# A pooling and latent-attention trunk: the attention's three engines in the order of the program text, with the projections cut into fine pieces

## The chip, the cores and the metric

The kernel runs on one core of one Trainium2 chip. The time is device microseconds of one execution; the median of some runs is compared. A core has TensorE (PE, matmuls and transposes), VectorE (DVE), ScalarE (ACT), GpSimd (POOL), SyncE (SP, which here only issues DMAs), an on-chip memory, and eight PSUM banks that matmuls write. Each engine executes its own list of instructions in the order in which the compiled program holds them; engines wait for each other by semaphores.

## What is computed

Two layers on 512 tokens of 2048 features, in float32. The first is a gated pooling mixer, which this change leaves as it is. After it come keys and values from a compressed latent of 512 and, from its own latent of 512, the queries of 16 heads of 128 + 64 features (the 64 are rotated by position):

```
q, k = qk_norm_rope(q, q_norm_g), qk_norm_rope(k, k_norm_g)   # per head: over 192 features
for i in range(4):                                            # query blocks of 128
    s = q[block i] @ k[: (i + 1) * 128].T * 192 ** -0.5       # chunks of 64 masked
    o[block i] = softmax(s) @ v[: (i + 1) * 128]
x = x + (o * silu(gate)) @ w_out
```

qk_norm_rope divides each token's 192 features by their root mean square. Block i sees i + 1 blocks of keys, so the work of a head grows from block 0 to block 3.

## The kernel before, in words

Every float32 operand is split in two parts of a faster type, hi (a cast, ScalarE) and lo (the difference, VectorE), and each product is three matmuls: hi hi, hi lo, lo hi. Weights are split too: `load_w` (line 118) loads 256 KB into one of three `raw` buffers (SP's queue) and makes a `whi` and a `wlo`, of which there are four each.

The mixer takes the first 1200 us or so. Then come the latents (`latent`, `latent_norm`), 16 gate projections (`gate_unit`, 599: 48 matmuls of 512 columns, Silu, the result kept in an `at` tile until its head is done), and the attention in eight head groups of two heads.

A group's preparation (`prep_units`, 813), in pieces with short names: B loads the k and v weights; k0 to k3 (`kv_unit`) make raw keys and values of four token blocks, 12 matmuls of 512 each; K (`kstats_unit`) makes the keys' reciprocal roots from sums of squares and scales the raw keys; q0 to q3 (`q_unit`, 12 matmuls of 384) make the raw queries; S (`qstats_unit`) their reciprocal roots. T0 to T5 (`tr_unit`, 709) are transposes of four 128 x 128 blocks into one PSUM bank each, which ScalarE and VectorE then empty with a cast and a difference: T0 and T1 the keys of two heads, T2 their rotated part (two banks), T3 and T4 the queries, T5 their rotated part.

The group's attention (`attn_units`, 826) has eight blocks (two heads, four blocks). `score_unit` (750) is five matmuls into a score bank, a mask (MEMSET), the maximum over the row, the exponential with its sum (ScalarE), a reciprocal and a scaling (VectorE). `pt_unit` (775) transposes the block's probabilities into a transpose bank and splits them; `pv_unit` (792) multiplies by v after every second block, and after the head's last one VectorE multiplies by the gate (line 811), into the gate's tile. `og_unit` splits a gated head, `out_unit` and `out_store` are the last projection.

PSUM: three banks `mm`, two `sc`, two `tr` (T0 to T5 and the probabilities' transposes take them in turn) and one `ov`.

The order around the attention: `main` is the list of blocks, `fill` the preparation of the next group (in the last group: parts of the last projection), and LEAD and PACE set how they mix. The program text is then reordered by a scheduler, which decides what stands where on each engine:

```
PREP = "B k0 k1 k2 k3 K q0 q1 T0 T2 q2 T1 q3 T3 T4 S T5".split()
...
        mpos += [hg + x / len(au) * PACE for x in range(len(au))]
...
        due += [hg + (x + 1) / n - LEAD for x in range(n)]
...
    while j < len(fill) and due[j] <= mpos[i]:
```

Of the kernel before, what the change touches and what calls it, by code (L numbers as in the profile page):

```python
# [43 lines left out]

PREP = "B k0 k1 k2 k3 K q0 q1 T0 T2 q2 T1 q3 T3 T4 S T5".split()

LEAD = 0.421
PACE = 1.091
# [3 lines left out]
def trunk_kernel(  # L52
# [27 lines left out]
    def at(dt=F32R):  # L80
        return apool.tile([P, S], dt, tag="a", name="at")
# [348 lines left out]
    xpool = ctx.enter_context(tc.tile_pool(name="xpool", bufs=16, **tile_))  # L430
# [35 lines left out]
    for g in range(NG):  # L466
# [11 lines left out]
        for o in range(KD):  # L478
            first = len(wloads)
            acc = proj(awo[g, o], 8, ys)  # L480
            if g == 0:
                x = xt()
# [117 lines left out]
    def gate_unit(o):  # L600
# [3 lines left out]
        sg = at(F32)  # L604
        A.activation(sg, z, AF.Silu)
        gates.append(sg)
# [5 lines left out]
    st = {}  # L612
# [4 lines left out]
    def hg_begin(hg):  # L617
        d = {}
        d["kvw"] = [load_w(wkvb[hg, :, k * 512:(k + 1) * 512], 512) for k in range(4)]
        d["kraw"] = [xt((P, 2, 256)) for _ in range(2)]  # L620
        d["qraw"] = [None] * 4
        vt = bt if hg else xt
        d["vh"] = [vt((P, 2, 256), F32R) for _ in range(2)]
        d["vl"] = [vt((P, 2, 256), F32R) for _ in range(2)]
# [4 lines left out]
    def kv_unit(hg, t):  # L629
        d = st[hg]  # L630
        acc = mm()
        tsl = slice(t * P, (t + 1) * P)
        for k in range(4):
            hi, lo = d["kvw"][k]
            ch, cl_ = cn[k]
            T.matmul(acc, ch[:, tsl], hi, start=(k == 0), stop=False)  # L636
            T.matmul(acc, cl_[:, tsl], hi, start=False, stop=False)  # L637
            T.matmul(acc, ch[:, tsl], lo, start=False, stop=(k == 3))  # L638
        a, b = t // 2, t % 2
        A.copy(d["kraw"][a][:, b, :], acc[:, 0:256])  # L640
        split(acc[:, 256:512], d["vh"][a][:, b, :], d["vl"][a][:, b, :])
        for h in range(2):
            junk = spool.tile([P, 192], mybir.dt.bfloat16, tag="junk", name="junk", bufs=2)
            A.activation(junk[:, 0:128], d["kraw"][a][:, b, h * P:(h + 1) * P], AF.Square,
                         accum_out=d["ssk"][:, 2 * t + h:2 * t + h + 1])

    def q_unit(hg, t):
        d = st[hg]
        if t == 0:
            d["qw"] = [load_w(wqb[hg, :, k * 384:(k + 1) * 384], 384) for k in range(4)]  # L650
        acc = mm()
        tsl = slice(t * P, (t + 1) * P)
        for k in range(4):
            hi, lo = d["qw"][k]
            qh, ql_ = qn[k]
            T.matmul(acc[:, 0:384], qh[:, tsl], hi[:, 0:384], start=(k == 0), stop=False)  # L656
# [156 lines left out]
    def prep_units(hg):  # L813
        def q(t):
            q_unit(hg, t)
            qrot_unit(hg, t)
# [154 lines left out]
```

## Time and profile before

| | us |
|---|---|
| median of three runs | 1948.48 (1948.02 to 1948.8) |
| the profiled execution | 1946.78 |
| its span, first to last instruction | 1945.0 |
| TensorE busy | 1920.2 |
| VectorE busy | 1276.3 |
| ScalarE busy | 822.6 |

The attention lies between 1500 and 1800 us of the span. In a row of the timeline the columns are start, duration, engine, line, operation, tiles (out<-in) and shapes; in square brackets the idle time of that engine just before and what ended it. A group row of the instructions ends in busy time, mean duration in ns, and idle time before. A row of the chain of waits is start, length, what. A row of a stretch has its length and each engine's busy time (instructions): PE, weight loads, DVE, ACT, POOL, then granted clock, DMA share and GB/s. A matmul's row shows its whole passage; the next one starts before it ends.

### The profile page before, as it was taken

The page shows a single profiled execution, that of the slowest core. Times are in us where ns is not written, and L with a number is a line of the kernel's source. Part 1 is how long each engine was busy: PE and PEld are TensorE (multiplying, and loading weights), DVE is VectorE, ACT ScalarE, POOL GpSimd, SP SyncE. Part 2 cuts the span into 40 slices and gives each one's busy share as a digit, 9 for nine tenths or more (in the row PEclk, how much of TensorE's full clock was granted, in tenths as well). Part 3 has the DMA queues.
Part 4 walks back from the last instruction along what each step waited for, and adds up shares of the span by engine and source line. Part 5 has one row for each costly group of instructions (what it writes and reads, how often), then busy time and mean ns, then how long its engine had stood idle before and what let it go on. Part 6 is the DMA issues. An engine that isn't in the chain of part 4 may idle for free.

```text
span 1945.0 us, 30576 instructions
## 1 busy us (share of the span) xinstructions
PE 1920.2 (99%) x11356; PEld 1707.8 (88%) x11356; DVE 1276.3 (66%) x2297; ACT 822.6 (42%) x1570; POOL 252.5 (13%) x404
## 2 busy tenths in 40 slices
PE   8999999999999999999999999999999999999999
PEld 8999999999999977888888888888888888888887
DVE  8677785896666687585685567473344888796432
ACT  7433433333333433333323454332244777785221
POOL 0423333343223000000000000000010111110000
PEclk9999999999999999999999999999999999999999
DMA  6545444344444446334334343333322111121632
GB/s 189 162 153 163 149 134 129 123 134 136 148 141 144 149 161 199 118 124 141 121 123 141 114 145 121 93 93 98 97 93 71 56 39 55 47 67 51 215 119 87
DMA packets 168006, 235.53 MB, mean 121 GB/s; under 512 B 14768, under 2 KB 95024, under 8 KB 167856
## 3 DMA queue, kind: packets, MB, share of 16 engines
q1 hardware_dynamic: 167568, 233.37, 37.8%
q8 instruction: 89, 1.46, 0.3%
q14 instruction: 61, 0.50, 0.1%
q10 hardware_dynamic: 288, 0.20, 0.0%
HBM read 208.35 MB, written 25.17 MB: 120 GB/s over the span
## 4 chain that ended last, share of the span: by engine, by line
PE 88%; DVE 4%; DMA 3%; ACT 3%; issue 1%; SPq 0%; POOL 0%; DVEq 0%; ACTq 0%; POOLq 0%
PE mm L147 14%; PE mm L146 14%; PE mm L145 14%; PE k L338 10%; PE k L334 10%; PE k L336 10%; PE sc L762 2%; PE mm L636 2%; PE mm L638 1%; PE mm L637 1%; PE mm L656 1%; PE mm L657 1%; PE mm L658 1%; PE tr L732 1%; DVE wlo L128 1%
## 5 line engine op out<-in xcount | busy, mean ns | idle before, releaser
L127 ACT CAST whi<-raw 128x512 fp32r<-128x512 f32 (+2 forms) x421 | 252.6, 608 | 505.2 <-PE mm L146 438.5
L334 PE MATMUL k<-xc,hi 128*128 128x256 f32 x1680 | 460.0, 283 | 0.0
L336 PE MATMUL k<-xc,hi 128*128 128x256 f32 x1680 | 460.0, 283 | 0.0
L128 DVE TENSOR_TENSOR wlo<-raw,whi 128x512 fp32r<-128x512 f32 (+2 forms) x421 | 281.4, 672 | 229.3 <-ACT whi L127 228.1
L338 PE MATMUL k<-xc,lo 128*128 128x256 f32 x1680 | 417.8, 283 | 1.1 <-DVE lo L316 1.0
L315 ACT CAST hi<-raw 128x1792 fp32r<-128x1792 f32 x120 | 202.7, 1689 | 363.0 <-PE k L338 246.2
L316 DVE TENSOR_TENSOR lo<-raw,hi 128x1792 fp32r<-128x1792 f32 x120 | 246.7, 2056 | 159.4 <-ACT hi L315 159.2
L147 PE MATMUL mm<-bt,wlo 128*128 128x512 f32 x860 | 335.9, 391 | 1.3 <-DVE wlo L128 1.3
L145 PE MATMUL mm<-bt,whi 128*128 128x512 f32 x860 | 334.9, 389 | 0.6 <-ACT bt L150 0.6
L146 PE MATMUL mm<-bt,whi 128*128 128x512 f32 x860 | 334.5, 389 | 0.0
L334 PEld LDWEIGHTS k<-xc,hi 128*128 128x128 f32 x1680 | 322.5, 192 | 0.0
L336 PEld LDWEIGHTS k<-xc,hi 128*128 128x128 f32 x1680 | 322.5, 192 | 0.0
L338 PEld LDWEIGHTS k<-xc,lo 128*128 128x128 f32 x1680 | 296.8, 192 | 2.0 <-DVE lo L316 1.5
L147 PE MATMUL mm<-at,wlo 128*128 128x512 f32 x516 | 201.3, 390 | 1.5 <-DVE wlo L128 1.5
L146 PE MATMUL mm<-at,whi 128*128 128x512 f32 x516 | 202.0, 392 | 0.2 <-DVE at L150 0.2
L145 PE MATMUL mm<-at,whi 128*128 128x512 f32 x516 | 200.7, 390 | 0.0
L147 PEld LDWEIGHTS mm<-bt,wlo 128*128 128x128 f32 x860 | 161.4, 188 | 36.7 <-DVE wlo L128 2.9
L145 PEld LDWEIGHTS mm<-bt,whi 128*128 128x128 f32 x860 | 161.4, 188 | 34.6 <-ACT bt L150 1.0
L146 PEld LDWEIGHTS mm<-bt,whi 128*128 128x128 f32 x860 | 161.4, 188 | 33.7 <-DVE bt L150 0.2
L311 POOL TENSOR_TENSOR raw<-raw 128x256 f32<-128x256 f32 x120 | 97.0, 808 | 436.4 <-DVE raw L309 413.4
L147 PEld LDWEIGHTS mm<-at,wlo 128*128 128x128 f32 x516 | 96.9, 188 | 22.5 <-DVE wlo L128 2.7
L146 PEld LDWEIGHTS mm<-at,whi 128*128 128x128 f32 x516 | 96.9, 188 | 21.3 <-DVE at L150 1.4
(1149 smaller groups left out, 2588.2 us busy)
## 6 DMA issues: line engine op xcount, KB each, us to landing
raw<-awin SPq DMA_DIRECT2D x240, 256.0 KB, 3.2
raw<-awo SPq DMA_DIRECT2D x128, 256.0 KB, 2.9
raw<-bwin SPq DMA_DIRECT2D x80, 256.0 KB, 2.8
raw<-awg SPq DMA_DIRECT2D x64, 256.0 KB, 2.7
raw<-bwo SPq DMA_DIRECT2D x59, 256.0 KB, 2.8
scr<-e SPq DMA_DIRECT2D x56, 256.0 KB, 2.7
raw<-wkvb SPq DMA_DIRECT2D x32, 256.0 KB, 2.9
raw<-wqb SPq DMA_DIRECT2D x32, 192.0 KB, 2.4
```

What stands on the lines that cost most here:

```text
L127: A.copy(hi[:, :n], raw[:, :n])
L128: V.tensor_tensor(lo[:, :n], raw[:, :n], f(hi[:, :n]), ALU.subtract)
L145: T.matmul(dst, wh, xh, start=first, stop=False)
L146: T.matmul(dst, wh, xl, start=False, stop=False)
L147: T.matmul(dst, wl, xh, start=False, stop=last)
L311: G.tensor_tensor(c[:, :, 6, :], c[:, :, 4, :], c[:, :, 2, :], ALU.add)
L315: A.copy(hi, c[:, :, 1:8, :])
L316: V.tensor_tensor(lo, c[:, :, 1:8, :], f(hi), ALU.subtract)
L334: T.matmul(dst, hi[:, j % 2, wi, :], xh[j][:, xi, :], start=first, stop=False, skip_group_check=True)
L336: T.matmul(dst, hi[:, j % 2, wi, :], xl[j][:, xi, :], start=False, stop=False, skip_group_check=True)
L338: T.matmul(dst, lo[:, j % 2, wi, :], xh[j][:, xi, :], start=False, stop=last, skip_group_check=True)
L636: T.matmul(acc, ch[:, tsl], hi, start=(k == 0), stop=False)
```

## The change

1. **The order.** After the first 14 gates, every instruction of TensorE, ScalarE and VectorE is bound behind the one that stands before it in the program text (`add_manual_dep`), so that the scheduler can't move it on its engine. DMAs and GpSimd aren't bound.
2. **The pieces.** k0 to q3 are cut into four pieces each (one weight chunk, three matmuls), the exponential, the scaling and the sums of squares become steps of their own. A list `prep_items` lays down the preparation; `fill_to` deals its pieces between the score blocks by time shares (0.35 and 0.7 of a block's slot), and continues without a break from one group into the next. K and S stay one piece each. Gates 14 and 15 are pieces of group 0's preparation, parts of the last projection those of the end.
3. **Weights.** A chunk is loaded and split in the text when the fourth last chunk was used for the last time.
4. **Buffers and DRAM.** The 16 `x` buffers are divided into 11 and 5 for queries; raw k and v use the `at` pool. A gate is stored to DRAM after its Silu, loaded two blocks before its head ends, multiplied, stored again (not for the last group) and loaded once more for its split: four transfers of 256 KB a head.

```diff
+    def kv_part(hg, t, k, w):
...
+        if k == 3:
+            a, b = t // 2, t % 2
+            split(acc[:, 256:512], d["vh"][a][:, b, :], d["vl"][a][:, b, :])
+            A.copy(d["kraw"][a][:, b, :], acc[:, 0:256])
...
+        first = [k(0, i) for i in range(4)]
+        for t in range(1, 4):
+            first += [k(t, 0), k(t, 1), kq(t - 1), k(t, 2), k(t, 3)]
...
+        first += [q(0, 0), q(0, 1), kq(3), q(0, 2), q(0, 3), piece(0, kstats_unit, hg),
+                  q(1, 0), q(1, 1), qq(0), q(1, 2), q(1, 3), kr(0), tr_(0), qq(1), tr_(1),
...
+        return (first + nxt[:2] + [qq(3), piece(0, qstats_unit, hg), tr_(3)] + nxt[2:3] + [tr_(4)] +
+                nxt[3:4] + [tr_(5)] + nxt[4:])
...
+    def fill_to(us):
+        nonlocal pos, done
+        while pos < len(fill) and done + fill[pos][0] / 2 <= us:
+            t, w, fn, a = fill[pos]
+            if w is None:
+                fn(*a)
+            else:
+                key = (fn, a[0], a[2]) if fn in (kv_part, q_part) else (fn,) + a
+                fn(*a, parts[key])
+            split_due(pos)
+            done += t
+            pos += 1
...
+    for m in range(len(seq) + 2):
+        now = seq[m] if m < len(seq) else None
+        if now:
...
+            score_unit(*now)
+        if m >= 2 and seq[m - 2][2] % 2:
+            pv_unit(*seq[m - 2][:2], seq[m - 2][2] // 2)
+        if now:
+            fill_to(at_ + share * 0.35)
+            exp_unit(*now)
+        if 1 <= m <= len(seq):
+            pt_unit(*seq[m - 1])
+        if now:
+            fill_to(at_ + share * 0.7)
+            scale_unit(*now)
+            fill_to(at_ + share)
...
+    for ins in block[begin:]:
+        e = ins.engine
+        if e in (mybir.EngineType.PE, mybir.EngineType.Activation, mybir.EngineType.DVE):
+            if e in prev:
+                tc.add_manual_dep(ins, prev[e].name, mybir.DependencyInfo(
+                    mybir.DependencyClass.NoSync, mybir.DependencyReason.DATA), reason="order of the pieces")
+            prev[e] = ins
```

What this does to the engines' lists is shown at three places of one head group in the middle; the other groups read alike. First VectorE before, at the end of the key statistics (`sy` is the reciprocal root, the eight rows of line 679 scale the raw keys, `sc` is a score bank, `nm` the maximum, `tr` a transpose bank):

```order
L164 SCALAR_TENSOR_TENSOR sy<-sa,sy 128x8
L679 TENSOR_SCALAR xt<-xt,sy 128x128 x8
L811 TENSOR_TENSOR at<-ov,at 128x512
L771 RECIPROCAL sm<-sm 128x1
L772 TENSOR_SCALAR tt__15897<-tt__15897,sm 128x128
L771 RECIPROCAL sm<-sm 128x1
L772 TENSOR_SCALAR tt__15935<-tt__15935,sm 128x256
L150 TENSOR_TENSOR bt<-tr,bt 128x512
```

and VectorE now, from the same step on:

```order
L163 SCALAR_TENSOR_TENSOR sy<-sa,sy 128x8
L692 TENSOR_SCALAR at<-at,sy 128x128 x8
L788 MEMSET sc 64x64
L790 TENSOR_REDUCE nm<-sc 128x1
L792 SCALAR_TENSOR_TENSOR nm<-nm,qy 128x1
L149 TENSOR_TENSOR xt<-tr,xt 128x2x128
L149 TENSOR_TENSOR xt<-tr,xt 128x128
L149 TENSOR_TENSOR bt<-tr,bt 128x512
L806 RECIPROCAL sm<-sm 128x1
L807 TENSOR_SCALAR tt__16571<-tt__16571,sm 128x512
L149 TENSOR_TENSOR bt<-tr,bt 128x512
```

The maximum of block 3 of the first head (L790) and the split of block 2's probabilities (the two L149 into `xt`) stand behind the scalings now; before, they stood elsewhere. ScalarE at the same place now (L800 is an exponential, L700 the rotated keys):

```order
L800 ACTIVATE tt__15415,sm<-sc,nm,qy 128x512
L149 CAST xt<-tr 128x2x128
L149 CAST xt<-tr 128x128
L670 COPY qt<-mm 128x384
L700 ACTIVATE tt__15439<-krr,sy 128x128 x4
L149 CAST bt<-tr 128x512
```

The cast of block 2's probabilities follows block 3's exponential, and T0's cast follows both. TensorE before, around one of these transposes (L732 is T0, T1, T3, T4 or T5, L656 to L658 the q projection):

```order
L656 MATMUL mm<-whi,at 128x384
L732 MATMUL tr<-cs,xt 128x128
L657 MATMUL mm<-whi,at 128x384
L732 MATMUL tr<-cs,xt 128x128
L658 MATMUL mm<-wlo,at 128x384
L732 MATMUL tr<-cs,xt 128x128 x2
L656 MATMUL mm<-whi,at 128x384
```

and TensorE now (L815 are the transposes of block 2's probabilities, L753 T0 and T1, L787 the scores of the second head's block 0):

```order
L815 MATMUL tr<-cs,tt__16485 128x128 x3
L664 MATMUL mm<-whi,at 128x384
L665 MATMUL mm<-whi,at 128x384
L666 MATMUL mm<-wlo,at 128x384
L753 MATMUL tr<-cs,at 128x128 x8
L787 MATMUL sc<-bt 128x128 x5
```

T0 and T1 are eight transposes in a row now, one q piece behind block 2's. And TensorE now at T3 and T4 (both L753):

```order
L753 MATMUL tr<-cs,qt 128x128 x4
L815 MATMUL tr<-cs,tt__16746 128x128 x2
L641 MATMUL mm<-whi,at 128x512
L642 MATMUL mm<-whi,at 128x512
L643 MATMUL mm<-wlo,at 128x512
L753 MATMUL tr<-cs,qt 128x128 x4
L641 MATMUL mm<-whi,at 128x512
```

Between T3 and T4 stand a block's two transposes and one k piece of the next group; the query statistics stand on VectorE between that block's scaling and T3's difference.

More of the change, by code (lines that the diff above doesn't have):

```diff
@@ L652, in q_unit @@
         tsl = slice(t * P, (t + 1) * P)
[L653 to L656, printed above, removed]
[L657 to L661 removed]
+        hi, lo = w
@@ new lines, in trunk_kernel, with split_due @@
+    for m, (key, w) in enumerate(keys):
+        n = last[keys[m - 4][0]] if m >= 4 else -1
+        assert n < use[key]
+        due.setdefault(n, []).append((key, w))
+    parts = {}
+    def split_due(n):
+        for key, w in due.get(n, ()):
+            parts[key] = load_w(*w)
+    block = nc.cur_bb.bb.instructions
+    begin = len(block)
+    split_due(-1)
+    pos, done = 0, 0.0
+    def fill_to(us):
[4 more added lines that the diff above has]
+                fn(*a)
+            else:
+                key = (fn, a[0], a[2]) if fn in (kv_part, q_part) else (fn,) + a
+                fn(*a, parts[key])
+            split_due(pos)
+            done += t
+            pos += 1
```

280 lines of the change are left out of this document (171 added, 109 removed).

## The prediction

> **What bounds the kernel now.** I read the page first, then the chain of waits, then TensorE's own rows. The page's busy line, and its slices:
>
> ```profile
> PE 1920.2 (99%) x11356; PEld 1707.8 (88%) x11356; DVE 1276.3 (66%) x2297; ACT 822.6 (42%) x1570; POOL 252.5 (13%) x404
> ...
> DVE  8677785896666687585685567473344888796432
> ...
> PEclk9999999999999999999999999999999999999999
> ```
>
> TensorE is the bound everywhere, and VectorE comes near it in the attention (0.7 to 0.9 in slices 32 to 36 of 40). The chain of waits passes TensorE once in each head group at the same place, so it shows the length of one group:
>
> ```profile
> 1584.04 2.02 PE sc L762 x10
> ...
> 1622.07 2.02 PE sc L762 x10
> ```
>
> A group takes 38.0 us. The stretch view says of one group:
>
> ```profile
> 1584.00:1622.00 38.00, 37.01 (x222) 32.66 (x221) 31.18 (x112) 28.37 (x98) 6.00 (x16) 1.00 0.16 50
> ```
>
> TensorE is busy for 37.0, VectorE for 31.2, ScalarE for 28.4 of 38.0 us. By busy time only 1.0 us could be won. But a matmul's row reaches past the start of the next. So I count starts: of 512 columns, 384, 256, and four transposes.
>
> ```profile
> 1608.20 0.39 PE L636 MATMUL mm<-whi,at 128*128 128x512 f32 x1
> 1608.42 0.39 PE L637 MATMUL mm<-whi,at 128*128 128x512 f32 x1
> ...
> 1613.79 0.33 PE L657 MATMUL mm<-whi,at 128*128 128x384 f32 x1
> ...
> 1615.70 0.33 PE L658 MATMUL mm<-wlo,at 128*128 128x384 f32 x1
> ...
> 1617.10 0.28 PE L806 MATMUL ov<-xt,bt 128*128 128x256 f32 x1
> ...
> 1617.69 0.28 PE L808 MATMUL ov<-xt,bt 128*128 128x256 f32 x1
> ```
>
> ```profile
> 1518.01 0.60 PE L732 MATMUL tr<-cs,xt 128*128 128x128 f32 x4
> 1518.36 0.60 PE L762 MATMUL sc<-bt 128*128 128x256 f32 x3
> ```
>
> That is 0.23, 0.174 (11 steps), 0.118 (5 steps), and 0.35 for four transposes. A group has 48 matmuls of 512 for k and v (10.9), 48 of 384 for q (8.3), the scores with 5 each of 128 to 512 for two heads (6.3), 36 for probabilities times v (4.0) and 48 transposes (4.2): 33.7 us. So **4.4 us** of each group's 38.0 are lost between starts. They lie in one stretch of 8 us, where no projection is left to run beside the softmax:
>
> ```profile
> 1600.68 0.39 PE L762 MATMUL sc<-bt 128*128 128x512 f32 x1
> 1601.31 0.55 PE L762 MATMUL sc<-bt 128*128 128x128 f32 x3 [0.24 <-ACT tt__16221 L770]
> ...
> 1605.37 0.28 PE L806 MATMUL ov<-xt,bt 128*128 128x256 f32 x1
> 1605.90 0.38 PE L807 MATMUL ov<-xt,bt 128*128 128x256 f32 x1 [0.25 <-DVE xt L150]
> ```
>
> 0.63 us stands where 0.23 would do, and 0.53 for 0.12. [...]
>
> **What the change removes.** It deals projection pieces evenly between the score blocks. If that worked without side effects it would win 4.4 us in each of seven groups, some 31 us, and a few more at both ends.
>
> **What it adds.** The three engines now run in the order of the program text. The statistics are one piece each there, and VectorE has nothing between their steps:
>
> ```profile
> 1614.28 0.16 DVE L162 TENSOR_TENSOR sa<-sy 128x8 f32<-128x8 f32 x1
> 1614.47 0.17 DVE L163 TENSOR_TENSOR sa<-sa,sv 128x8 f32<-128x8 f32 x1
> ...
> 1615.27 0.17 DVE L164 SCALAR_TENSOR_TENSOR sy<-sa,sy 128x8 f32<-128x8 f32 x1
> 1615.47 1.66 DVE L679 TENSOR_SCALAR xt<-xt,sy 128x128 f32<-128x128 f32 x8
> ```
>
> Steps that wait for each other start 0.20 us apart (1614.28 to 1615.27 is five of them). The key statistics have 11 such steps (2.2), four small additions before them (some 0.5) and eight scalings (1.66): 4.4 us. The query statistics have 12 steps: 2.4 us. Other durations, of one group, come from the groups of instructions with their shapes:
>
> ```profile
> L150 ACT CAST xt<-tr 128x256 fp32r<-128x256 f32 x8 | 3.0, 376 | 0.5 <-PE tr L781 0.5
> ...
> L150 ACT CAST xt<-tr 128x128 fp32r<-128x128 f32 x4 | 1.1, 264 | 1.2 <-PE tr L781 1.2
> ```
>
> ```profile
> L150 DVE TENSOR_TENSOR xt<-tr,xt 128x256 fp32r<-128x256 f32 x8 | 3.3, 416 | 0.3 <-ACT xt L150 0.3
> ...
> L150 DVE TENSOR_TENSOR bt<-tr,bt 128x512 fp32r<-128x512 f32 x3 | 2.1, 693 | 1.2 <-ACT bt L150 1.2
> ...
> L745 DVE SCALAR_TENSOR_TENSOR bt<-tr,gqk,bt 128x512 fp32r<-128x512 f32 x2 | 1.5, 746 | 0.1
> ...
> L765 DVE TENSOR_REDUCE nm<-sc 128x1 f32<-128x512 f32 x2 | 1.4, 678 | 0.0
> ...
> L767 DVE SCALAR_TENSOR_TENSOR nm<-nm,qy 128x1 f32<-128x1 f32 x8 | 1.2, 146 | 0.0
> ...
> L150 DVE TENSOR_TENSOR xt<-tr,xt 128x128 fp32r<-128x128 f32 x4 | 1.1, 284 | 0.0
> ...
> L765 DVE TENSOR_REDUCE nm<-sc 128x1 f32<-128x384 f32 x2 | 1.1, 554 | 0.0
> ```
>
> and from ScalarE's and VectorE's rows around one exponential:
>
> ```profile
> 1603.75 0.78 ACT L770 ACTIVATE tt__16282<-sc,nm,qy 128x512 f32<-128x512 f32 x1
> 1604.41 0.21 ACT L770 ACTIVATION_READ_ACCUMULATOR tt__16282<-sc,nm,qy 128x1 f32 x1
> 1604.50 0.37 ACT L150 CAST xt<-tr 128x256 fp32r<-128x256 f32 x1
> ```
>
> ```profile
> 1604.65 0.16 DVE L771 RECIPROCAL sm<-sm 128x1 f32<-128x1 f32 x1
> 1604.92 0.49 DVE L772 TENSOR_SCALAR tt__16282<-tt__16282,sm 128x512 f32<-128x512 f32 x1
> ```
>
> An exponential of 512 holds ScalarE for 0.75 us, and a handoff costs 0.03 (accumulator done at 1604.62, reciprocal at 1604.65). Now TensorE's new waits in a group, one by one.
>
> *T1, the second key transpose.* On TensorE it follows T0 at once. It needs the transpose bank that block 2's probabilities hold (there are two banks). These leave through ScalarE and VectorE, in turns, and both engines have other work ahead of that: VectorE the key statistics and then block 3's maximum, ScalarE block 3's exponential. T0 ends when the seventh scaling is done. From there: the eighth scaling 0.20, maximum 0.68, its scaling 0.15, exponential 0.75, cast 0.38, difference 0.42, second cast 0.26, difference 0.28 = 3.1, with handoffs **3.3 us** in which TensorE has nothing in its order. That holds however late the engines come. Low 3.1, high 3.5.
>
> *T0 itself.* From the end of block 2's scores TensorE has eight q pieces (24 x 0.174), block 3's scores (1.1), a product (0.65) and five block transposes (0.5): 6.4 us. VectorE and ScalarE need maximum 0.55 + 0.15, exponential some 0.66, cast 0.38, difference 0.42, reciprocal and scaling some 0.6, statistics until T0 4.2: 7.0, with handoffs 7.4. So 1.0 at least. And in VectorE's order the split of the fourth q weight stands ahead of that maximum:
>
> ```profile
> raw<-wqb SPq DMA_DIRECT2D x32, 192.0 KB, 2.4
> ```
>
> Its load waits for a raw buffer that the first q weight leaves (three buffers), which waits for the last use of the first k weight. Cast and split 0.5 each, 2.4 landing, 0.5 each again is 4.4 after a point that lies 2.8 before the end of block 2's scores: the maximum comes some 1.6 late. I take **2.6** (1.0 to 2.7), and 0.4 for the q piece that waits for that weight.
>
> *T4, the second query transpose.* It needs T3's bank; T3's difference stands behind the query statistics, and these behind block 2's maximum. Maximum 0.55 + 0.15, statistics 2.4, difference 0.75 and handoffs: 4.0 us, against two block transposes and one k piece on TensorE (0.9): **3.0** (2.3 if TensorE is late).
>
> *T2.* After block 3's scaling VectorE makes T1's difference (0.69), the maximum of 128 columns and its scaling (0.4), the exponential 0.45, then cast, difference, cast, difference (1.6): 3.2, 3.4 with handoffs, before a bank is free; TensorE has 1.2 of work. **2.1** (1.0 to 2.3).
>
> *Block 3's transposes*, twice a group: once behind T0's cast, 0.5; once behind T4, two T5 halves, k splits and its own exponential, some 9.4 us of alternating work against 7.0 on TensorE: 2.3. Together **2.8** (0 to 3).
>
> Sum per group: 3.3 + 2.6 + 0.4 + 3.0 + 2.1 + 2.8 = **14.2 us** lost in place of 4.4; bounds 7.8 and 15.5. Seven groups: 7 x 9.8 = +69.
>
> **The rest.** Projection of group 0 stands alone now, with gates 14 and 15 inside: statistics 4.4 against 2.1 us of q pieces before T0, and the query statistics once: some 4 us lost. I put the loss there now at 2, an estimate by the same count of starts: +2 (0 to +5). Group 7 with output pieces: such a piece is four weights long (2.7 us), VectorE's load is lighter; I give it and the ends -4 (-6 to +3), since the loss there now can go. DRAM trips: four transfers of 256 KB a group on queues that are 0.16 busy; a gate load is issued two blocks (8 us) before its product. Their cover is that lead; without it a landing, 2 to 3 us a head, would show, so 0 (0 to +10). The new buffers and the other order of cast and copy move nothing ahead of a matmul: 0.
>
> Sum: the profiled execution took 1946.78 us (span 1945.0 and 1.78 around it, 1.7 below the median). 1946.78 + 69 + 2 - 4 = 2013.8; I take **2012**, a little off for idle engines that answer sooner.
>
> **Rivals.** *Only the bounds hold* (18%). If T0, T2 and the block transposes wait little because the engines catch up, 7.8 a group remain: 7 x 3.4 = +24, 1970. Speaking for it: VectorE would be busy for only 31 of some 47 us.
>
> *The clock falls as well* (15%). At the start, after 5.8 us of idle time, 256 columns took 0.21 us instead of 0.12, and 4 us later still did:
>
> ```profile
> 5.80 0.58 PE L387 MATMUL k<-xc,hi 128*128 128x256 f32 x1 [5.80 <-ACT hi L150]
> ...
> 9.59 0.41 PE L388 MATMUL k<-xc,hi 128*128 128x256 f32 x1
> 9.80 0.41 PE L387 MATMUL k<-xc,hi 128*128 128x256 f32 x1
> ```
>
> Four us at that rate hold work for a little over two, so a fall costs some 2 us. T0's and T1's waits lie 0.35 us apart, 6 us of little work. One fall a group is 7 x 2 = +14: 2026. [...] No row here shows a fall in the middle of the kernel: the granted clock is in its highest tenth in every slice.
>
> *Faster* (11%). The even dealing wins and the waits stay under 4.4 us a group. This needs the statistics to be out of the way before TensorE comes to T0 and T3: VectorE would have to reach them 5 us sooner than worked out, and T1's wait would have to be a chain that I read wrongly. With 1 us left a group: 7 x -3.4 - 4 = 1919. For it: VectorE has 31 us of work for 33.7 on TensorE, so there is room on paper. Against it: the order is fixed, and VectorE can't go ahead in it. It decides at 4.4 us of waits a group.
>
> *The change cancels itself* (4%): waits of about 4.4, 1945.
>
> **Numbers.** Forecast 52%. A difference under 0.2% (3.9 us) is about what can't be told from none. Slower 52 + 18 + 15, and 1 of the last: 0.86; same 0.03; faster 0.11. The range leaves out the faster case and little above: bounds of the sum are 1960 and 2025, with the clock 2036: 1958 to 2036.
>
> **What would show it.** In the profile after: the distance of equal places of two groups near 47.5 us; rows of the second key transpose with over 3 us of idle time before, ended by VectorE's difference; TensorE's busy share in the attention down from 97% to some 75%; VectorE's busy time a group still 31 us; no change before the gates. I am wrong if groups take under 38 us, or if the waits are ended by DMAs.

## The result, and the profile after

| | before | after |
|---|---|---|
| median, us | 1948.25 (4 runs, 1947.73 to 1948.8) | 2057.89 (4 runs, 2056.18 to 2058.4) |
| span of the profiled execution | 1945.0 | 2055.7 |
| a head group in the steady part | 38.0 | 51.2 |

The ratio is 1.0561, with a 95% interval of 1.0543 to 1.0579: slower by 109.6 us. The forecast was 2012 with a range of 1958 to 2036. The direction was right, the size was not.

The page of the changed kernel, busy line, VectorE's slices and the granted clock:

```profile
PE 1961.6 (95%) x11356; PEld 1735.4 (84%) x11356; DVE 1300.5 (63%) x2297; ACT 828.0 (40%) x1570; POOL 253.0 (12%) x404
...
DVE  8677776886666774866845666533466666666432
...
PEclk9999999999999999999999999999989888889999
```

VectorE's slices in the attention (30 to 37 of 40) are at 0.6 where 0.7 to 0.9 stood, and the clock, which was in its highest tenth all the time before, is mostly at 0.8 there. One group in the stretch view (length, then busy time of PE, weight loads, DVE, ACT, POOL, the granted clock, DMA share, GB/s):

```profile
1631.80:1683.00 51.20, 41.75 (x222) 36.08 (x221) 34.11 (x111) 28.92 (x96) 6.44 (x16) 0.87 0.18 57
```

No engine is full: TensorE 82%, VectorE 67%, ScalarE 56%. TensorE's own rows of this group, from T1 of the group before it to T0 and T1 of its own (L753 are T0, T1, T3 and T4; L736 is T2; L815 transposes probabilities, with x1 to x4 for block 0 to block 3; a row of L753 at the edge of a view can show fewer than its four):

```profile
1626.93 0.88 PE L753 MATMUL tr<-cs,at 128*128 128x128 f32 x3 [3.24 <-DVE xt L149]
...
1633.81 0.63 PE L736 MATMUL tr<-cs,tt__16063 128*128 128x128 f32 x4 [0.92 <-DVE xt L149]
...
1645.39 1.12 PE L753 MATMUL tr<-cs,qt 128*128 128x128 f32 x4 [2.72 <-DVE bt L766]
...
1646.73 0.63 PE L642 MATMUL mm<-whi,at 128*128 128x512 f32 x1
1647.16 0.63 PE L643 MATMUL mm<-wlo,at 128*128 128x512 f32 x1
...
1651.82 0.40 PE L642 MATMUL mm<-whi,at 128*128 128x512 f32 x1
1652.06 0.40 PE L643 MATMUL mm<-wlo,at 128*128 128x512 f32 x1
...
1655.95 0.60 PE L815 MATMUL tr<-cs,tt__16310 128*128 128x128 f32 x4
...
1670.31 0.49 PE L815 MATMUL tr<-cs,tt__16485 128*128 128x128 f32 x3
...
1670.99 0.34 PE L666 MATMUL mm<-wlo,at 128*128 128x384 f32 x1
1673.57 1.41 PE L753 MATMUL tr<-cs,at 128*128 128x128 f32 x4 [2.24 <-DVE at L692]
1678.22 1.09 PE L753 MATMUL tr<-cs,at 128*128 128x128 f32 x4 [3.24 <-DVE xt L149]
...
1680.07 0.63 PE L664 MATMUL mm<-whi,at 128*128 128x384 f32 x1
1680.49 0.52 PE L665 MATMUL mm<-whi,at 128*128 128x384 f32 x1
```

The four waits stand where the prediction put them: T2's second half (0.92, ended by the difference of block 3's probabilities), T4 (2.72, by T3's difference), T0 (2.24, by a key scaling) and T1 (3.24, by the difference of block 2's probabilities). Block 3's transposes (1655.95) don't wait at all. After T4's and after T1's wait the starts stand wide apart: 0.43 us for 512 columns (1646.73 to 1647.16) where 0.23 is the rate before and afterwards (1651.82 to 1652.06). That is the low clock: granted 0.50 from 1644.47 to 1651.28 and 1.00 in the 3.41 us behind.

Counted by starts as in the prediction, this group loses 17.7 us: 10.3 in the waits (T1 3.5, T4 2.9, T0 2.4, T2 1.1, block 1's transposes 0.4; each is the idle time and its start), 0.8 because T0's four transposes follow the scalings at 0.4 us each, 4.9 in the two stretches of low clock (1645.39 to 1651.21: 5.82 us for 2.88 us of work; 1678.22 to 1682.06: 3.84 for 1.84), and 1.7 in small gaps. By stages:

| stage | lost before | lost after | more | the prediction's term |
|---|---|---|---|---|
| group 0's projection alone (1440 to 1484; before: 1416 to 1434) | 0.0 | 5.2 | 5.2 | +2 |
| the seven stretches from T2 to T2 | 34.8 | 123.5 | 88.7 | +69 |
| after the last T2 | 3.5 | 18.8 | 15.3 | -4 |

That is 109 of 110.7 us between the two spans. By the rates that one takes for the shapes, such a count can be off by some 0.2 us a stretch.

Why T1 waits can be read row by row. VectorE:

```profile
1673.14 1.66 DVE L692 TENSOR_SCALAR at<-at,sy 128x128 f32<-128x128 f32 x8
1674.80 0.11 DVE L788 MEMSET sc<- 64x64 f32 x1
1674.94 0.69 DVE L790 TENSOR_REDUCE nm<-sc 128x1 f32<-128x512 f32 x1
1675.67 0.16 DVE L792 SCALAR_TENSOR_TENSOR nm<-nm,qy 128x1 f32<-128x1 f32 x1
1677.03 0.42 DVE L149 TENSOR_TENSOR xt<-tr,xt 128x256 fp32r<-128x256 f32 x1 [1.20 <-ACT xt L149]
1677.78 0.29 DVE L149 TENSOR_TENSOR xt<-tr,xt 128x128 fp32r<-128x128 f32 x1 [0.33 <-ACT xt L149]
```

and ScalarE in the same time:

```profile
1670.18 0.19 ACT L677 ACTIVATION_READ_ACCUMULATOR junk<-qt 128x1 f32 x1
1675.86 0.78 ACT L800 ACTIVATE tt__16571<-sc,nm,qy 128x512 f32<-128x512 f32 x1 [5.49 <-DVE nm L792]
1676.54 0.19 ACT L800 ACTIVATION_READ_ACCUMULATOR tt__16571<-sc,nm,qy 128x1 f32 x1
1676.63 0.36 ACT L149 CAST xt<-tr 128x256 fp32r<-128x256 f32 x1
1677.48 0.27 ACT L149 CAST xt<-tr 128x128 fp32r<-128x128 f32 x1 [0.49 <-DVE xt L149]
```

Block 2's probabilities were in the transpose bank at 1670.8 (the row at 1670.31 above). ScalarE was free then (its row at 1670.18 ends at 1670.4), but its next instruction was block 3's exponential, and it sat 5.49 us before that, because the maximum stood behind the key statistics on VectorE. VectorE then sat 1.20 us for the cast. Each of the two engines was idle because of the order of the other.

### The profile page after: what moved, and what is told of

Its sections match the earlier page's. It is cut to its first block, busy times and chain, and to the rows that moved or that the text cites. A ratio compares the mean times of both kernels' runs of the same rounds, so it can differ in the third digit from the quotient of the medians.

```text
span 2055.7 us, 30705 instructions
## 1 busy us (share of the span) xinstructions
PE 1961.6 (95%) x11356; PEld 1735.4 (84%) x11356; DVE 1300.5 (63%) x2297; ACT 828.0 (40%) x1570; POOL 253.0 (12%) x404
## 5 line engine op out<-in xcount | busy, mean ns | idle before, releaser
L144 PE MATMUL mm<-bt,whi 128*128 128x512 f32 x944 | 368.2, 390 | 2.8 <-ACT bt L149 2.8
L146 PE MATMUL mm<-bt,wlo 128*128 128x512 f32 x944 | 368.7, 391 | 1.5 <-DVE wlo L127 1.5
L145 PE MATMUL mm<-bt,whi 128*128 128x512 f32 x944 | 367.7, 390 | 0.1
L144 PEld LDWEIGHTS mm<-bt,whi 128*128 128x128 f32 x944 | 177.3, 188 | 40.6 <-ACT bt L149 3.7
L146 PEld LDWEIGHTS mm<-bt,wlo 128*128 128x128 f32 x944 | 177.3, 188 | 39.7 <-DVE wlo L127 2.7
L145 PEld LDWEIGHTS mm<-bt,whi 128*128 128x128 f32 x944 | 177.3, 188 | 37.5 <-DVE bt L149 0.9
L146 PE MATMUL mm<-at,wlo 128*128 128x512 f32 x432 | 169.1, 391 | 1.4 <-DVE wlo L127 1.4
L145 PE MATMUL mm<-at,whi 128*128 128x512 f32 x432 | 169.7, 393 | 0.3 <-DVE at L149 0.2
L144 PE MATMUL mm<-at,whi 128*128 128x512 f32 x432 | 169.2, 392 | 0.0
L310 POOL TENSOR_TENSOR raw<-raw 128x256 f32<-128x256 f32 x120 | 98.5, 821 | 439.8 <-DVE raw L308 423.3
L311 POOL TENSOR_TENSOR raw<-raw 128x256 f32<-128x256 f32 x120 | 98.9, 824 | 9.2
L146 PEld LDWEIGHTS mm<-at,wlo 128*128 128x128 f32 x432 | 81.5, 189 | 19.3 <-DVE wlo L127 2.3
```

The source lines that it names most:

```text
L144: T.matmul(dst, wh, xh, start=first, stop=False)
L145: T.matmul(dst, wh, xl, start=False, stop=False)
L146: T.matmul(dst, wl, xh, start=False, stop=last)
L310: G.tensor_tensor(c[:, :, 6, :], c[:, :, 4, :], c[:, :, 2, :], ALU.add)
L311: G.tensor_tensor(c[:, :, 7, :], c[:, :, 6, :], c[:, :, 3, :], ALU.add)
```

## The experiments

Theory: a group's length is a chain that goes through VectorE's lumps of statistics and its turns with ScalarE, in an order that neither engine can leave. Following the rows back from T1 to the T1 before it, each to what released it, some 26 us of the 51.3 lie on VectorE and ScalarE (17.1 from 1661.13 to 1678.22, 7.5 from 1637.88 to 1645.39, and 1.8 before T2's second half), the rest on TensorE. The chain leaves TensorE at 1637.9 and at 1661.1 for the cast of a weight, which waits (1.07 and 0.76 us) until TensorE has used its `whi` buffer for the last time. Rivals: the low clock; banks; TensorE's order; trips and pools. No run changed the weights' buffers, so what these add stays open.

The group's length is the median of six distances from T2 to T2. "Apart" means other places for T0 to T5, described below.

| | median, us | against before (95%) | group, us |
|---|---|---|---|
| changed kernel | 2057.9 | 1.0543 to 1.0579 | 51.2 |
| TensorE kept busy | 2058.5 | 1.0544 to 1.0575 | 51.3 |
| T0, T1, T3 in other banks | 2039.9 | 1.0450 to 1.0481 | 49.0 |
| order for TensorE alone | 1991.9 | 1.0205 to 1.0235 | 44.2 |
| shorter lumps | 2040.3 | 1.0458 to 1.0492 | 48.8 |
| no order laid down | 1971.9 | 1.0099 to 1.0129 | 44.0 |
| no trips through DRAM | 2056.1 | 1.0528 to 1.0563 | 51.2 |
| order for TensorE and VectorE | 2049.5 | 1.0492 to 1.0534 | 50.1 |
| T0 to T5 apart, all three orders | 2026.8 | 1.0376 to 1.0418 | 47.7 |
| apart, order for TensorE alone | 1947.0 | 0.9989 to 1.0007 | 36.9 |
| the same, less on VectorE | 1950.0 | 1.0003 to 1.0021 | 37.9 |
| short output pieces | 2050.0 | 1.0514 to 1.0543 | 51.4 |
| apart, TensorE alone, short output pieces | 1948.7 | 1.0002 to 1.0020 | 36.7 |

**Is it the low clock?** TensorE is kept busy in three of the waits:

```
+        nf = {0: 8, 1: 12, 4: 10}.get(u, 0) if hg else 0
+        if nf:
+            z = mm()
+            for j in range(nf):
+                T.matmul(z, cn[0][0][:, 0:P], cn[1][0], start=True, stop=True)
         p = tr()
```

> The changed kernel, with matmuls of 512 columns whose result nobody reads put ahead of three transposes of each of groups 1 to 7: 8 ahead of T0, 12 ahead of T1, 10 ahead of T4 (30 x 0.227 = 6.8 us of extra work a group, a little less than the 2.2, 3.2 and 2.7 us that TensorE stands still there). Nothing else changes. Theory (the waits are chains on VectorE and ScalarE, and the low clock that follows them is a cost of its own): the starts stay at 0.227 us after the waits, the 0.43 us rows are gone, a group gets some 5 us shorter (51.2 to about 46) and the time is 7 x 5 = 35 us lower, about 2022. Rival (VectorE's chain sets the group's length, a quicker TensorE only waits longer): 2058, within 6, and longer waits at T0 and T4. Rival (the slow rows are not the clock but contention): the rows stay at 0.43 and the time rises to 2060 to 2080.

2058.47. TensorE's rows of one group (lines moved by five: L758 is T4, T0 and T1, L820 the probabilities, L749 the filler):

```profile
1633.09 0.63 PE L736 MATMUL tr<-cs,tt__16151 128*128 128x128 f32 x4 [1.71 <-DVE xt L149]
...
1644.69 0.66 PE L758 MATMUL tr<-cs,qt 128*128 128x128 f32 x4 [0.44 <-DVE bt L771]
...
1654.68 0.63 PE L820 MATMUL tr<-cs,tt__16409 128*128 128x128 f32 x4 [2.01 <-DVE sc L793]
...
1656.31 0.63 PE L641 MATMUL mm<-whi,at 128*128 128x512 f32 x1
1656.73 0.63 PE L642 MATMUL mm<-whi,at 128*128 128x512 f32 x1
...
1673.90 1.41 PE L758 MATMUL tr<-cs,at 128*128 128x128 f32 x4 [0.37 <-DVE at L692]
1675.07 3.00 PE L749 MATMUL mm<-at 128*128 128x512 f32 x12
1678.55 0.63 PE L758 MATMUL tr<-cs,at 128*128 128x128 f32 x4 [0.48 <-DVE xt L149]
```

The clock stays up where it fell, and nothing is won. The mean granted clock goes from 0.975 to 0.992. In its place block 3's transposes wait 2.01 us (with a fall of its own in some groups, here 1656.31 to 1656.73), and T2 1.71 for 0.92; the groups take 50.3 and 51.9 us in turn. So my theory, which gave the low clock a price of its own, fell at this point: the slower TensorE had only hidden the wait that comes next. The chain through the other two engines is as long without it. The rival that expected longer waits "at T0 and T4" had the time right and the places wrong.

**Banks.** T0, T1 and T3 get banks that no probabilities hold:

```
-        p = tr()
+        p = mm() if u in (0, 1, 3) else tr()
```

> The changed kernel, with T0, T1 and T3 in banks of the projections (three of them) and no longer in the two transpose banks; T2, T4, T5 and the probabilities stay there. The order of the pieces is the same. Theory (T1 and T4 wait for a bank whose reader stands behind the statistics and the exponential): 3.4 us before T1 and 2.9 us before T4 go, about 1.5 come back before T2, whose bank block 2's probabilities hold, 0.5 before T5; with no wait over 2.5 us the clock stays up, some 4 us more. 4 + 4 = 8 to 9 us a group, 7 x 9 = 63: about 1995. Rival (VectorE's work between T0 and T2 is the bound, and the wait only moves to the next tile that it must deliver): under 1 us a group, 2050 to 2058, with 4 us or more before T2.

2039.88. TensorE (L753 x8 at 1665.53 is T0 and T1 together, the one at 1639.54 is T5):

```profile
1639.54 0.63 PE L753 MATMUL tr<-cs,tt__15927 128*128 128x128 f32 x4 [2.03 <-DVE xt L149]
...
1665.53 2.42 PE L753 MATMUL mm<-cs,at 128*128 128x128 f32 x8 [2.25 <-DVE at L692]
...
1670.15 0.69 PE L664 MATMUL mm<-whi,at 128*128 128x384 f32 x1 [1.24 <-ACT qt L670]
```

T1's 3.24 and T4's 2.72 are gone, as the theory had it; but 1.24 came back before the next q piece, 2.03 before T5 and 1.51 before block 3's transposes, and T2's wait rose from 0.92 to 1.80, of 6 us saved. The wait before the q piece ends with ScalarE's copy out of a projection bank: it is a cost of the edit itself, which takes these banks for the transposes. The clock didn't stay up either (0.984 in the mean). The group wins 2.2: nearer to the rival (the wait moves on) than to my 1995.

**Whose order?** First the order of TensorE alone, then none, then TensorE and VectorE:

```
-        if e in (mybir.EngineType.PE, mybir.EngineType.Activation, mybir.EngineType.DVE):
+        if e in (mybir.EngineType.PE,):
```

> The changed kernel with the order laid down for TensorE alone; VectorE and ScalarE are ordered by the scheduler, which puts the steps of the statistics between other work. TensorE's order in the groups is the same. Theory (lumps in a fixed order are what T4 waits for; T0 and T1 wait for the key scalings and for block 2's probabilities, which are still behind block 3's maximum there): the 2.9 us before T4 and the 3 us of low clock behind it go, T0 and T1 stay within 1 us: 7 x 5 = 35 less, about 2022. Rival (the fixed order of VectorE and ScalarE causes all of it): the waits go together, 1940 to 1960. Rival (TensorE's own order, T1 right behind T0 and T4 so close to T3, causes it): 2050 to 2065.

1991.89, twice the saving that the theory expected:

```profile
1616.70 0.55 PE L753 MATMUL tr<-cs,qt 128*128 128x128 f32 x3 [0.70 <-DVE bt L766]
...
1641.13 1.42 PE L753 MATMUL tr<-cs,at 128*128 128x128 f32 x4 [0.31 <-DVE at L692]
1645.91 0.85 PE L753 MATMUL tr<-cs,at 128*128 128x128 f32 x4 [3.36 <-DVE bt L149]
```

T4 waits 0.70 and T0 0.31, and the low clock behind T4 is gone (a group's granted clock is 0.92 to 0.96 for 0.87): 2.0 + 1.9 + 2.9 = 6.8 of the 7.0 us a group. T0's share is what I had not expected. T1's 3.36 stays. The ends get shorter too: after the last T2 this run loses 3.1 us, about as before the change (3.5; in the changed kernel 18.8), and in group 0's projection 1.1 for 5.2.

```
-        if e in (mybir.EngineType.PE, mybir.EngineType.Activation, mybir.EngineType.DVE):
+        if e in ():
```

> The changed kernel without the order laid down: the scheduler orders all three engines; the pieces, the pools, the trips through DRAM and the program text are the same. Theory (the fixed order is what costs; of the 51.2 us of a group, 7 went when VectorE and ScalarE were freed, and 3.6 before T1 with about 1 of low clock stay because TensorE's own order puts T1 right behind T0): the rest goes too, a group of about 40 us, 1992 - 7 x 4.5 = 1960. Rival (pieces, pools and trips cost something by themselves, whatever the order): 1980 or more. Rival (without the order the even dealing wins as meant): under 1940.

1971.9, between the theory and its first rival, so this run doesn't decide whether pieces and trips cost something; the one with both edits, below, does.

```
-        if e in (mybir.EngineType.PE, mybir.EngineType.Activation, mybir.EngineType.DVE):
+        if e in (mybir.EngineType.PE, mybir.EngineType.DVE):
```

> The changed kernel with the order laid down for TensorE and VectorE; ScalarE alone is ordered by the scheduler. With TensorE alone laid down it took 1992, with all three 2058. Theory (VectorE's order, with the statistics as lumps ahead of the maximum and of the split that others wait for, is most of it): 2030 to 2055, T4's wait still 2 us or more. Rival (ScalarE's order, the exponential ahead of the casts that free a bank, is most of it): 1990 to 2010.

2049.5: of the 66 us between the order for one engine and for three, adding VectorE's alone makes 58. T4 waits 2.84 there, T1 3.54, and the loss after the last T2 is back at 17.7 us. No run laid down the order of TensorE and ScalarE without VectorE's, so what ScalarE's order costs by itself isn't known.

**Lumps.** One step of the reciprocal root instead of three:

```
-    def rsqrt(v, y, a, n):
+    def rsqrt(v, y, a, n, steps=3):
...
-        for _ in range(3):
+        for _ in range(steps):
...
-        rsqrt(v, y, a, 8)
+        rsqrt(v, y, a, 8, 1)
```

> The changed kernel with one step of the reciprocal root in place of three in the key and query statistics: six instructions of 0.20 us fewer in each of the two lumps (the values are less exact). Theory (the lumps are on the way to T0 and T4, not to T1's wait, which begins after them): 1.2 us less before T0 (2.4 to 1.2), 1.2 less before T4 (2.9 to 1.7), T1's 3.4 stays within 0.3. 7 x 2.4 = 17: 2041; if a wait of 1.7 us no longer lowers the clock, another 3 a group, 2020. Rival (banks and ScalarE set these waits, the lumps are beside them): 2052 to 2058, all three waits within 0.3.

2040.34. T4, block 3's transposes, T0 and T1:

```profile
1683.56 0.66 PE L753 MATMUL tr<-cs,qt 128*128 128x128 f32 x4 [1.52 <-DVE bt L766]
...
1693.55 0.63 PE L815 MATMUL tr<-cs,tt__16828 128*128 128x128 f32 x4 [2.01 <-DVE sc L788]
...
1710.00 1.41 PE L753 MATMUL tr<-cs,at 128*128 128x128 f32 x4 [1.03 <-DVE at L692]
1714.66 0.66 PE L753 MATMUL tr<-cs,at 128*128 128x128 f32 x2 [3.25 <-DVE xt L149]
```

2.72 to 1.52, 2.24 to 1.03, and 3.24 to 3.25: the lumps are on the way to T4 and T0 in full, and T1's wait begins after them. 2.4 us off VectorE's lumps is 2.4 us off the group. Behind T4 the low clock went in most groups (four of six; 0.983 in the mean for 0.975), and block 3's transposes wait 2.01 in its place, as with the filler.

**Trips through DRAM.**

```
-            gt = d[("G", h)] = bt(dt=F32)
-            nc.sync.dma_start(gt, gates[2 * hg + h])
+            d[("G", h)] = bt(dt=F32)
...
-            V.tensor_tensor(gt, ov, gt, ALU.mult)
+            V.tensor_tensor(gt, ov, f(cn[0][0]), ALU.mult)
-            if hg < nhg - 1:
-                nc.sync.dma_start(gates[2 * hg + h], gt)
```

> The changed kernel without the trips of the attention through DRAM: the gate isn't loaded back (the product takes a resident tile in its place) and the gated head isn't stored, so the values are not the reference's; the gates are still stored before the attention and loaded for the output pieces. VectorE's instructions are the same. Theory (the trips are hidden): 2058, within 5. Rival (SP's queue, on which a store that waits for VectorE stands ahead of the weight loads, delays the weights): 10 to 30 lower, with the q piece that waits for its weight and the casts earlier.

2056.11 (2053.74 to 2059.46), the same waits to 0.01 us (2.72, 2.23, 3.24), the same 51.2 us a group. The attention's trips are hidden.

**TensorE's places.** The key scalings in two halves, T0 to T5 at other places (a table now gives the place of each, in pieces of the group):

```
+POS = dict(kq3=17, K=19, S0=21, S1=23, R0=23, T0=24, R1=25, T1=26, T20=27, T21=29,
+           qq0=21, qq1=24, qq2=28, qq3=33, Q=33, T3=36, T4=38, T5=40)
```

> All three orders laid down as in the changed kernel, but the key scalings split in two halves, one a head, and the transposes moved: T0 after one q piece more, T1, T2 and its second half two or more q pieces apart, T3, T4 and T5 each two k pieces apart (three after the query statistics). Theory (the group's length is a chain that goes through VectorE's lumps and its turns with ScalarE, 30 of 51 us of it, and only its TensorE parts and T1's bank can be moved away): T1's wait under 1.5 us, T4's under 2, no low clock, but new waits at the probabilities' transposes; a group of 45 to 48 us, 2005 to 2030. Rival (the places of T0 to T5 on TensorE are all that is wrong): the waits go with nothing in their place, 38 us a group, 1965 or lower.

2026.81. No wait before T0 or T1 above 0.2 us, and in their place (L819 transposes probabilities):

```profile
1654.53 0.41 PE L819 MATMUL tr<-cs,tt__16469 128*128 128x128 f32 x2 [2.50 <-DVE tt__16469 L811]
...
1677.75 0.41 PE L819 MATMUL tr<-cs,tt__16805 128*128 128x128 f32 x2 [2.12 <-DVE tt__16805 L811]
```

TensorE now waits for the scaled probabilities themselves. The theory held for the waits, the group and the time: places and halved scalings are worth 3.5 us a group as long as VectorE's order is fixed. It was wrong on the clock, which falls behind these two waits (0.987 in the mean; behind the second, 512 columns take 0.43 us again, 1679.72 to 1680.15).

Both edits together, T0 to T5 apart and the order for TensorE alone:

```
-        if e in (mybir.EngineType.PE, mybir.EngineType.Activation, mybir.EngineType.DVE):
+        if e in (mybir.EngineType.PE,):
```

> The two edits before put together: T0 to T5 apart as in the run with all three orders laid down (2027), but the order laid down for TensorE alone (with the changed kernel's places that took 1992). Theory (two causes that each hide what the other one gives: VectorE's fixed order, and T1 and T4 close behind T0 and T3 on TensorE): neither the waits before T0, T1 and T4 nor those before the probabilities' transposes stay above 1.5 us each, no low clock, a group of 37 to 40 us, 1940 to 1960. Rival (fine pieces and trips cost some 20 us whatever the order, as in the run without any order, 1972): 1965 to 1985.

1946.98, the time of the kernel before (1947.0 beside it). The stretch view of one group, and T0, T1 and T2 in TensorE's rows (L757, L740):

```profile
1583.40:1620.30 36.90, 35.98 (x221) 32.46 (x221) 31.98 (x112) 28.72 (x97) 6.09 (x16) 1.00 0.25 80
```

```profile
1614.96 0.60 PE L757 MATMUL tr<-cs,at 128*128 128x128 f32 x4
...
1618.25 0.62 PE L757 MATMUL tr<-cs,at 128*128 128x128 f32 x4
...
1620.28 0.66 PE L740 MATMUL tr<-cs,tt__16553 128*128 128x128 f32 x4 [0.55 <-DVE bt L150]
```

The group takes 36.9 us, 1.2 less than before, the clock is 1.00, and TensorE is busy for 36.0 of 36.9. So the fine pieces, the pools and the trips together cost no more than the even dealing wins, against the rival's 20 us; the dealing does win in the groups, though 1.2 and not 4.4 us each. The time over all is no better, and the count of starts says where the gain goes. The five steady stretches from T2 to T2 lose 15.9 us where 22.5 were lost before. But group 0's projection, the first and the last of the seven stretches and the rest of the kernel lose 0.6 + 6.0 + 7.3 + 4.7 = 18.6, where it was 0.0 + 4.3 + 6.7 + 3.2 = 14.2. In the last stretch T0 waits 2.39 us; the granted clock of this execution is 0.999 in the mean. That leaves some 2 us in this profile, which is of the fastest of ten executions (1943.08), and nothing in the median.

The same with less on VectorE (head 1's key scalings on GpSimd, five instructions of the key statistics in one, T0, T1 and T2 a little later):

```
-        for t in range(4):
-            V.tensor_scalar(v[:, 2 * t:2 * t + 2], d["ssk"][:, 2 * t:2 * t + 2], kr2[:, t:t + 1], None, ALU.add)
-        V.tensor_scalar(v, v, 1.0 / 192, EPS, ALU.mult, ALU.add)
+        V.scalar_tensor_tensor(v, d["ssk"], 1.0 / 192, kr8, ALU.mult, ALU.add)
...
+            if h:
+                G.tensor_tensor(kk, kk, y[:, c:c + 1].broadcast_to([P, P]), ALU.mult)
```

> As the run before, with less on VectorE: the four additions and the scaling of the key statistics in one instruction (five became one, some 0.9 us), and the four key scalings of head 1 on GpSimd (0.8 us off VectorE, 0.46 us each there); T0, T1 and the first half of T2 one or two q pieces later. Theory (VectorE's work is what is left of the bound, 32 to 34 us of a group): 1 to 1.5 us less a group, 7 to 10 us under the run before, 1930 to 1950. Rival (TensorE's 33.7 us of starts are the bound by then): no more than 3 us less.

1950.02, 3 us more and not less. VectorE's rows of a group add up to 35.4 us for 37.1, as said, and it is busy for 31.3 us a group for 32.0; but a wait of 1.47 us before T2 came in its place, and the group got 1.1 longer. Places and work were changed at once here, so which of them did it stays open.

**The last group.** Output pieces of one weight each:

```
-        return [(0.69 * n, (bwo[...], n * P), out_part, (o, k0, n))]
+        return [(0.69, (bwo[...], n * P), out_part, (o, k0, j)) for j in range(n)]
```

In the changed kernel a whole piece of 12 matmuls stands ahead of a block's scores, and nothing between these and the transposes of the block before, which then wait:

```profile
1846.52 0.39 PE L146 MATMUL mm<-at,wlo 128*128 128x512 f32 x1
1846.75 1.06 PE L787 MATMUL sc<-bt 128*128 128x384 f32 x5
1849.60 0.41 PE L815 MATMUL tr<-cs,tt__18523 128*128 128x128 f32 x2 [1.79 <-DVE sc L788]
```

> The changed kernel with the output pieces of the last group one weight long (0.69 us) where they were four (2.7 us); the same matmuls, weights loaded as before, all three orders laid down. In the changed kernel the stretch after the last group's first T2 loses 19.0 us between TensorE's starts (before: 3.7), in waits of 1 to 2 us before the probabilities' transposes, where all of a piece stands ahead of the scores and nothing between them and the transposes. Theory (coarse pieces leave the softmax of a block uncovered): the loss there falls to 8 to 12, the time by 7 to 11, 2047 to 2051. Rival (VectorE's fixed order, with the splits of the gated heads and the query statistics ahead of the softmax, sets these waits): 2054 to 2060.

2050.0: the time is as the theory had it, and the loss after the last T2 went from 18.8 to 12.8 us, a little above its 8 to 12. Coarse pieces are not the whole cause, though: with the order for TensorE alone the same pieces of four weights lose 3.1 us there. It takes VectorE's fixed order, the rival's cause, to make them cost. And on the kernel with T0 to T5 apart and one order:

> The same edit on the kernel with T0 to T5 apart and the order laid down for TensorE alone (1947, the time of the kernel before). It loses 5 us after the last T2. Theory (coarse pieces cost where VectorE can't go ahead; here it can): no more than 4 us lower, 1943 to 1948. Rival (the fine pieces gain what they gain with all orders laid down): 1936 to 1940.

1948.69: no gain, as the theory said of it (the time is 0.7 above its range). No version tried here beats the kernel before.

## Why the prediction was right and wrong

**The waits** were worked out from VectorE's and ScalarE's order by the durations in the rows of before, and three of the six terms came out to within half a microsecond: T1 3.3 (3.24 measured; the rows above are the sum's terms one by one but for the first, since the eighth scaling ends at 1674.80, before T0's row does), T4 3.0 (2.72), T0 2.6 (2.24, and 0.8 more between its own transposes). The key statistics with their scalings took 5.2 us and not 4.4; the four small additions alone took 1.1 where 0.5 was put. The q piece that was to wait 0.4 for its weight didn't wait. The trips at 0 were right.

**T2 and block 3's transposes** (2.1 and 2.8) came out at 0.92 and nothing. The reasoning was near for a TensorE at full clock: with the filler they are 1.71 and 2.01. In the changed kernel the low clock ahead of them hides them. The first of the six groups with a T4 wait shows the same: there the low clock behind T4 lasted half as long (3.41 us for 6.83), and block 3's transposes waited 1.12 us.

**The sum per group failed in size**: "Sum per group ... = 14.2 us lost in place of 4.4". It was 17.7. The 4.4 of before was a total that held every small gap; the 14.2 held six named waits only. These were 11.1 us in all (T0's 0.8 among them), the small gaps 1.7, and the low clock 4.9. The low clock was put at nothing in the sum; it stood beside it as a rival, as one fall a group at 2 us, with no row of before that shows a fall behind a wait of 2.7 us, and it fell twice. With the filler the group is as long without these two falls, so the low clock is where the time shows, and the length comes from the chain through VectorE and ScalarE. The step that failed is thus the adding itself: waits at single places, put on top of TensorE's work at full rate. A sum of this kind asks of each wait what is late there; the period of a fixed order is the length of the chain once around. That is 3.5 us a group, 20 us of the miss. The shorter lumps bear the chain out (2.4 us off VectorE's work took 2.4 off the group), and so does freeing VectorE and ScalarE (7.0).

**The ends failed outright**: "Group 7 with output pieces: such a piece is four weights long (2.7 us), VectorE's load is lighter; I give it and the ends -4". It was +15.3, some 19 us of the miss. I had the fact (pieces of 2.7 us) and drew the wrong conclusion from it; short pieces took 8 us off the time. And VectorE's lighter load didn't help, since its order was fixed there as well: with that order free, the same pieces lose 3.1 us. Group 0's projection alone lost 5.2 and before nothing, just above the bounds of that term (0 to 5) and 3 more than the 2 taken. The range was too narrow by its own bounds: 1946.8 + 7 x 11.1 + 5 + 3 and a fall of the clock a group (14) make some 2046, not 2036.

**The signs named beforehand**: the distance was to be 47.5 and was 51.2; rows of T1 with over 3 us, ended by VectorE's difference: yes; TensorE's busy share 75%: 82%, since rows at the low clock are longer; VectorE's busy time 31 us: 34.1. As many instructions (111 in each) add up to 36.9 us of rows for 35.8 before; the rest of the rise is overlap, 2.8 us of these rows where it was 4.5, since a row that follows a wait doesn't overlap the row before.

**The direction** rested on one sentence, that VectorE can't go ahead in a fixed order. The runs bear it out: adding VectorE's order makes 58 of the 66 us that the order on the two other engines costs, and with both of these freed and the transposes apart the kernel is back at 1947.

## What to carry to other kernels

Where several engines run in one fixed order, follow the chain once around through all of them, rather than adding waits to the work of the busiest: an idle engine may be the one that the others' order holds up, and a wait that is taken away can reappear at the next handoff (with the filler T1's 3.24 us went to 0.48, and block 3's transposes waited 2.01 for nothing before). If the order of one engine is fixed, let the others be ordered by what is ready: that was worth 66 us here. Whether it pays to fix the first one isn't shown: with the places of the changed kernel no order at all (1972) was better than TensorE's alone (1992), and with the better places no run left TensorE free. Ahead of work that others wait for, a run of dependent small instructions cost its whole length here: 2.4 us less of them made a group 2.4 us shorter. Look at the first and the last round by themselves, with the size of the pieces that are left to cover them there.

## What the hardware showed that was not expected

The clock fell behind less idle time than I had taken: the rival in the prediction set 6 us of little work beside the 5.80 us of idle time at the start, and in the changed kernel it fell behind waits of 2.72 us. Nor did the length of one wait tell here whether it falls. In the profile of the changed kernel the granted clock first falls, after the start, at 1480.62, and all its later changes lie whole multiples of 3.41 us from there. Four neighbouring steps of that length around T4's wait (1642.67 to 1645.39); the granted clock is the number behind POOL's:

```profile
1641.05:1644.46 3.41, 1.42 (x8) 0.73 (x6) 2.98 (x16) 1.72 (x4) 0.60 (x2) 1.00 0.48 151
1644.47:1647.87 3.40, 2.48 (x9) 2.08 (x10) 1.77 (x5) 0.73 (x2) 0.00 (x0) 0.50 0.00 0
1647.88:1651.28 3.40, 3.40 (x13) 2.92 (x12) 1.80 (x6) 1.75 (x4) 0.00 (x0) 0.50 0.00 0
1651.28:1654.69 3.41, 3.41 (x22) 2.97 (x22) 1.92 (x5) 1.30 (x5) 0.00 (x0) 1.00 0.00 0
```

TensorE is busy for 1.42 of 3.41 us in the first step; the granted clock is 0.50 in the next, while T4 still waits, and 1.00 again after a step that is full. Counted over this profile in such steps (its first 60 and its last 5 us left out), a fall followed 17 of the 553 steps at full clock, with 1.11 to 1.63 us of busy time each, and none of the other 536, which hold 1.81 or more. In the kernel before, the granted clock is 1.00 from 20 to 1940 us. At 0.50, 512 columns take 0.43 us for 0.23.

So waits of one length were followed by it at one place and not at another. T4's waits of 2.72 us in the changed kernel were followed by the low clock six times out of six, but a group of 51.2 us is 15 steps, so they all lie at nearly the same place among them. In group 0's projection a wait of 1.22 us (1477.66 to 1478.89) lies within one step with 1.63 us of busy time, and the clock is 0.50 from 1480.62; in the last group a wait of 1.79 us (1847.81 to 1849.60) goes over the end of a step at 1849.25, the two steps hold 1.91 and 3.06 us of busy time, and the clock stays at 1.00. With the filler, waits of 2.01 us were followed by it four times and twice not, and waits of 1.71 us never; with the shorter lumps, waits of 1.52 us twice out of six. And around T1 the low clock begins 0.2 us into T1's wait (at 1675.18): the step before, with 1.28 us of busy time, holds most of T0's wait.

T0 shows another thing: transposes that follow four pairs of scalings start 0.4 us apart (1673.87, 1674.26 and 1674.65 in the changed kernel), the pace of the scalings (eight in 1.66 us), and the idle time in their row (2.24) holds none of that.
